# Channel means of a transformer block: two float32r passes over a split sum in place of one float32 product

## The chip, the cores and the metric

The kernel runs on one core of a Trainium2 chip. The metric is the device time of one execution in microseconds (us). The kernel before took 987.19 us, the median of three runs (986.78 to 987.68).

A core has a matrix engine (TensorE, PE in the profile; PEld is its loading of weights), a vector engine (VectorE, DVE), a scalar engine (ScalarE, ACT), a general engine (GpSimd, POOL), and queues that move data by DMA (SyncE, SP, issues most of them). Each engine takes its own instructions in one order, and waits on the others through semaphores. Matrix results land in PSUM, in banks of 128 x 512 float32.

## The reference, cut to what matters

One layer over 512 positions of 1024 channels: a normalised input is projected and goes through three mixers (a spatial gating unit, a convolution with LayerNorm, a pooling), which are merged by gates and projected; then a feed-forward part and a gated embedding follow.

```python
def rms_norm(x, g):
    y = x * lax.rsqrt(jnp.mean(x * x, axis=-1, keepdims=True) + EPS)
    return y * g
def layer_norm(x, g, b):
    mu = jnp.mean(x, axis=-1, keepdims=True)
    xc = x - mu
    var = jnp.mean(xc * xc, axis=-1, keepdims=True)
    return xc * lax.rsqrt(var + EPS) * g + b
def reference(...):
    hn = rms_norm(h, g_mix_pre)
    z_sgu, z_conv, z_pool, z_gate = jnp.split(hn @ w_in, SPLITS, axis=-1)
    br_a = spatial_gating(gelu(z_sgu), ...) @ w_sgu_out
    br_b = conformer_conv(z_conv, ...) @ w_conv_out   # GLU, conv of 31 taps, layer_norm, silu
    br_c = multiscale_pool(z_pool, ...) @ w_pool_out
    merged = gates[0] * br_a + gates[1] * br_b + gates[2] * br_c
    h = h + rms_norm(merged @ w_out, g_mix_post)
    hn = rms_norm(h, g_ffn_pre)
    f = (silu(hn @ w_gate) * (hn @ w_up)) @ w_ffn_out
    h = h + rms_norm(f, g_ffn_post)
    return h + sigmoid(h @ w_ple_gate) * (p @ w_ple)
```

## The kernel before

The activations lie transposed: channels on the 128 partitions, in eight tiles, and the 512 positions along the free dimension. A weight block of 128 outputs is loaded, split into two float32r halves (a cast on ScalarE gives the high half, a subtraction on VectorE the low half; that is `split`), and stays in TensorE while the positions stream past. Every float32 product is three float32r passes (`mm3`): high by high, high by low, low by high. Two blocks are loaded and split ahead of use; tiles `raw`, `hi`, `lo` (and `w_hi`, `w_lo` in other slots) hold them.

A norm needs a mean over the channels, and channels lie on partitions. The squares of the eight tiles are first added up (`x_sums`, `conv_sum`, `var_sum`, `o_sums`, `h_sums`, `f_sums`, each 128 partitions wide), on VectorE or POOL. Then `channel_mean` multiplies the sum by a 128 x 128 matrix of 1/1024 (`mean_mat`), which gives the mean on every partition in the one PSUM bank `ps_stat`. This is the only product in plain float32. `inv_rms` puts eight VectorE instructions behind it (`rsqrt`, tiles `x_inv`, `o_inv`, `h_inv`, `f_inv`, `conv_inv`, `rs_t`).

There are eight such means. Four have 512 positions: `x_sums` (first norm, multiplied in behind the first products `ps_first`), `conv_sum` and `var_sum` (mean and variance of the LayerNorm of the convolution, while TensorE computes the gate tiles `ps_gate`; tiles `acc` hold the convolution, `conv` its halves afterwards, which `ps_br` needs), and `h_sums` (norm ahead of the feed-forward part). Four have 256, since the norm behind the output projection (`o_sums`) and the last norm (`f_sums`) are done for each half of the positions, so that the norm and the residual of one half run beside products of the other. In the code of these two, and of the feed-forward start between them, work is written by hand in the order in which it is meant to run, inside `with order():`. Every VectorE, ScalarE and TensorE instruction written there (through `dve`, `act_e`, `pe`) is kept behind all those that were written before it. Outside, a scheduler places the instructions by a model of the time. The background taps of the convolution (`drain`) are in written order too.

In the post-norm the order is: four output tiles for all positions; the last four for the first half; the first of these for the second half; the mean of the first half; then the others, with the residual of the first half (`res.tile`) between them; a part of the feed-forward products (`ps_f`); the eight squares of h in the first half (`square_h`); the mean of the second half; its residual; and the rest of the products. In the last norm: the last tile's first half is finished, its mean taken after a few products of the second half, then the embedding products `ps_ple` with the first half's residual between them, two slices of the last product `ps_pg`, and the mean of the second half.

In the profile nearly all instructions carry line 69, the helper that records them, so tiles tell them apart; L281 is the addition of squares on POOL.

Of the kernel before, what the change touches and what calls it, by code (L numbers as in the profile page):

```python
# [8 lines left out]
F32 = mybir.dt.float32  # L9
F32R = mybir.dt.float32r  # L10
# [6 lines left out]
P = 128  # L17
T = 512
H = 256
D = 1024  # L20
# [18 lines left out]

# The first GLU pairs are multiplied before the norm of x is known.  # L40
N_RAW = 3
N_FIRST = 2 * N_RAW * P
# Matrix products on nothing that raise the tensor engine's clock while the first loads run.
N_WARM = 8
# Taps of the depthwise convolution for each tile of GLU, v, gate a, pooling, gate c; and of u.
TAPS = (4, 3, 5, 3, 5)
TAPS_U = 4
# Where a norm or a piece of a residual goes between the products, counted in k-tiles.
STAT_K, STAT_A, STAT_H, STAT_F = 4, 2, 7, 2
# [5 lines left out]
class InOrder:  # L55
    """Engines whose instructions, while `on`, are issued behind all those written before them."""

# [24 lines left out]
def hybrid_block(  # L82
# [3 lines left out]
):  # L86
    """Activations live transposed (channels on partitions, the 512 positions free), so that every
    weight is a stationary operand as it lies in memory and is loaded once. A float32 product is
    three float32r passes: each operand is split exactly into a high and a low half of 12 bits."""
    nc = tc.nc  # L90
    order = InOrder(tc)
    dve, act_e, pe = order.engine(nc.vector), order.engine(nc.scalar), order.engine(nc.tensor)

    const = ctx.enter_context(tc.tile_pool(name="const", bufs=1))
    stream = ctx.enter_context(tc.tile_pool(name="stream", bufs=3))
    wide = ctx.enter_context(tc.tile_pool(name="wide", bufs=2))
    act = ctx.enter_context(tc.tile_pool(name="act", bufs=8))
# [18 lines left out]

# [1 line left out]
    vec = const.tile([P, N_VEC + WIDTH * KT], F32, name="vec")  # L118
# [24 lines left out]

    mean_mat = const.tile([P, P], F32, name="mean_mat")
    dve.memset(mean_mat, 1.0 / D)
    warm = const.tile([P, 1], F32, name="warm")
    act_e.copy(warm, mean_mat[:, :1])
    warm_up = const.tile([P, T], BF16, name="warm_up")
# [11 lines left out]

# [1 line left out]
    def split(hi, lo, src):  # L162
# [3 lines left out]
    def split_scaled(hi, lo, src, scale):  # L166
        """The halves of src * scale, scale one number per partition."""
        act_e.activation(out=hi, in_=src, func=AF.Copy, scale=scale)
        dve.scalar_tensor_tensor(out=lo, in0=src, scalar=scale, in1=hi,
                                       op0=ALU.mult, op1=ALU.subtract)  # L170
# [34 lines left out]
    weights = Weights()  # L205
# [9 lines left out]
    def product(ps, w, acts, hs=FULL, k0=0, last=True):  # L215
        """ps[n, t] (+)= sum over the block's k of w[k, n] act[k, t]."""
        hi, lo = w
        for i, a in enumerate(acts):
            mm3(ps[:, hs], blk(hi, i), blk(lo, i), a[:, 0, hs], a[:, 1, hs],
                k0 + i == 0, last and i == len(acts) - 1)  # L220
# [7 lines left out]

# [1 line left out]
    background = []  # L230
# [6 lines left out]
    def rsqrt(y, a, t):  # L237
        """y = 1 / sqrt(a): a bit-pattern guess, a Newton step scaled by S, a third-order step."""
        dve.tensor_scalar(out=y.bitcast(I32), in0=a.bitcast(I32), scalar1=-0.5,
                          scalar2=RSQRT_SEED, op0=ALU.mult, op1=ALU.add)  # L240
        dve.tensor_tensor(out=t, in0=y, in1=y, op=ALU.mult)
        dve.scalar_tensor_tensor(out=t, in0=t, scalar=-RSQRT_C2 * RSQRT_S, in1=a,
                                 op0=ALU.mult, op1=ALU.mult)
        dve.scalar_tensor_tensor(out=y, in0=t, scalar=RSQRT_C1 * RSQRT_S, in1=y,
                                 op0=ALU.add, op1=ALU.mult)
        dve.tensor_tensor(out=t, in0=y, in1=y, op=ALU.mult)
        dve.tensor_tensor(out=t, in0=t, in1=a, op=ALU.mult)
        dve.scalar_tensor_tensor(out=t, in0=t, scalar=-10.0 / 3.0 * RSQRT_S ** 2, in1=t,
                                 op0=ALU.add, op1=ALU.mult)
        dve.scalar_tensor_tensor(out=y, in0=t, scalar=5.0 * RSQRT_S ** 4, in1=y,  # L250
                                 op0=ALU.add, op1=ALU.mult)

    def channel_mean(sums):
        """The mean over the channels of what `sums` holds by partition, on every partition."""
        ps = psum.tile([P, T], F32, tag="pst", name="ps_stat", bufs=1)
        ps = ps[:, :sums.shape[1]]
        pe.matmul(ps, lhsT=mean_mat, rhs=sums, start=True, stop=True)
        return ps

    def inv_rms(sums, y):  # L260
        """y = 1 / sqrt(mean over the channels + eps), on every partition; eps is in the sums."""
        rsqrt(y, channel_mean(sums), t2("rs_t", sums.shape[1]))
# [6 lines left out]
    def add_square(sums, src, i, engine):  # L269
        """The i-th of the squares that are summed; the second brings eps along."""  # L270
        if i == 0:
            act_e.activation(out=sums, in_=src, func=AF.Square)
        else:
            add_sq(sums, square(src), i, engine)
# [7 lines left out]

# [1 line left out]
    C_U, C_V, C_A, C_G, C_P, C_M = 0, 8, 16, 24, 32, 40  # L284
# [56 lines left out]

# [1 line left out]
    xg = [slot("br", f"xg{k}") for k in range(KT)]  # L343
    x_sums = row("x_sums")
    first = []
# [13 lines left out]

# [1 line left out]
    h_conv = [slot("cv", f"h_conv{i}", F32) for i in range(4)]  # L361
# [67 lines left out]

# [1 line left out]
    def natural(dst, evacuate, taps):  # L431
        """dst[t, block, c] from z with the positions on partitions; yields behind each block."""
        for c in range(2):
            banks = [bank("ps_nat") for _ in range(NB)]
            for kk in range(4):
                hi, lo = weights.get()
                for b in range(NB):
                    ts = slice(b * P, (b + 1) * P)
                    for j in range(2):
                        k = 2 * kk + j  # L440
                        a = hn[k]
                        ws = slice(j * T, (j + 1) * T)
                        pe.matmul(banks[b], lhsT=a[:, 0, ts], rhs=hi[:, ws],
                                         start=k == 0, stop=False)
                        pe.matmul(banks[b], lhsT=a[:, 1, ts], rhs=hi[:, ws],
                                         start=False, stop=False)
                        pe.matmul(banks[b], lhsT=a[:, 0, ts], rhs=lo[:, ws],
                                         start=False, stop=k == KT - 1)
                drain(taps)
                if kk == 3:  # L450
                    for b in range(NB):
                        evacuate(dst, b, c, banks[b])
                yield c, kk
# [73 lines left out]

# [1 line left out]
    merged = wide_tile("merged")  # L529
# [25 lines left out]

# [1 line left out]
    z_all = wide_tile("z_all")  # L557
# [44 lines left out]
    gates = []  # L602
# [12 lines left out]

# [1 line left out]
    drain(len(background))  # L617
# [31 lines left out]

    # ---- output projection, post-norm, residual; the last tiles a half of the positions at a time,  # L650
    # so that the norm of one half runs behind the product of the other ----
    o_all = wide_tile("o_all")
# [4 lines left out]
    class Residual:  # L657
        """h += o * y tile by tile, and the halves of h * scale; the low half runs a tile behind."""

# [49 lines left out]
    with order():  # L709
# [23 lines left out]

# [1 line left out]
        banks = [bank("ps_f") for _ in range(2 * N_PAIR)]  # L735
# [92 lines left out]
    with order():  # L828
# [26 lines left out]

# [1 line left out]
        w_ple_1 = weights.get(0)  # L857
# [31 lines left out]
def _blocks(w):  # L889
    """[K, N] -> [N / 128, 128, K]: one block for each 128 outputs, its k-tiles side by side."""  # L890
    k, n = w.shape
    return w.reshape(k // P, P, n // P, P).transpose(2, 1, 0, 3).reshape(n // P, P, k)


def _wide_blocks(w):
    """[1024, 1024] -> [8, 128, 1024]: for each half of the outputs, pairs of k-tiles."""
    return w.reshape(4, 2, P, 2, T).transpose(3, 0, 2, 1, 4).reshape(8, P, D)
# [54 lines left out]
```

## Time and profile before

| what | value |
|---|---|
| median of three runs | 987.19 us (986.78 to 987.68) |
| profiled execution, first to last instruction | 984.9 us |
| TensorE busy | 974.1 us (99%) |
| VectorE, ScalarE, POOL busy | 675.5, 347.1, 87.4 us |
| chain that ended last | TensorE 89%, VectorE 7% |
| granted TensorE clock | 1.000 |

The page gives busy times, the chain of waits that ended last, and the costliest groups of instructions. A row of the timeline has the start in us, the length in us, the engine, the operation, output and inputs, shapes, how many instructions were merged (x), and in brackets how long the engine had been idle before, and what ended it. A row of the chain has start, length and what was running. Products overlap in their records: how long one holds TensorE is seen from the starts that follow, or from a long stretch divided by its count. The profile has 2.3 us less than the median of the runs, since it counts from the first to the last instruction.

### The profile page before, as it was taken

Reading aid. Unit: us, or ns where it says so; the run is one execution under the profiler, and the core shown is the slowest. Engines: PE = TensorE matmul, PEld = TensorE weight load, DVE = VectorE, ACT = ScalarE, POOL = GpSimd, SP = SyncE. Lnnn points to the kernel's source line nnn. Section 1 sums busy time; section 2 is a strip of 40 time slices with the busy share of each in tenths; the row PEclk is TensorE's granted clock in tenths of the full one; section 3 lists DMA queues with packets and bytes.
Section 4 is the critical chain, followed back from the end, with each engine's and each line's share of the span. In section 5 each row is a group of like instructions: output and inputs, shape, how many; then the busy total and the mean of one; then the engine's idle time right before and its main releaser. Section 6 shows DMA issues by size and latency. Waiting matters only on the chain.

```text
span 984.9 us, 11718 instructions
## 1 busy us (share of the span) xinstructions
PE 974.1 (99%) x4682; PEld 818.4 (83%) x4682; DVE 675.5 (69%) x903; ACT 347.1 (35%) x483; POOL 87.4 (9%) x64
## 2 busy tenths in 40 slices
PE   9999999899999999999999999999999999999998
PEld 6788888688888788888888998888888888888897
DVE  7998789998988799967556687554445442223675
ACT  6422333332223332246426443332232322223442
POOL 4000004000003702160000010000000000000000
PEclk9999999999999999999999999999999999999999
DMA  6433331322222232231328102323222333334312
GB/s 226 143 107 107 109 106 65 106 69 103 86 97 86 76 128 86 102 113 65 116 99 277 65 25 74 116 86 107 88 105 87 104 84 107 93 92 141 107 43 86
DMA packets 30006, 100.53 MB, mean 102 GB/s; under 512 B 3456, under 2 KB 3968, under 8 KB 29952
## 3 DMA queue, kind: packets, MB, share of 16 engines
q1 hardware_dynamic: 29808, 99.75, 30.2%
q8 instruction: 36, 0.59, 0.2%
q14 instruction: 18, 0.15, 0.0%
q10 hardware_dynamic: 144, 0.04, 0.0%
HBM read 97.68 MB, written 2.10 MB: 101 GB/s over the span
## 4 chain that ended last, share of the span: by engine, by line
PE 89%; DVE 7%; issue 2%; DMA 1%; ACT 1%; SPq 0%; DVEq 0%; ACTq 0%
PE ps_f L69 24%; PE ps_gate L69 13%; PE ps_br L69 13%; PE ps_fo L69 12%; PE ps_ag L69 5%; PE ps_pg L69 5%; PE ps_o L69 5%; PE ps_nat L69 4%; PE ps_z L69 4%; DVE lo L69 2%; DVE acc L69 1%; PE ps_pool L69 1%; PE ps_ple L69 1%; DVE v_all L69 1%; DMA first_all<-in_w_first 1%
## 5 line engine op out<-in xcount | busy, mean ns | idle before, releaser
L69 ACT CAST hi<-raw 128x1024 fp32r<-128x1024 f32 (+3 forms) x158 | 162.5, 1030 | 455.6 <-PE ps_br L69 88.4
L69 DVE TENSOR_TENSOR lo<-raw,hi 128x1024 fp32r<-128x1024 f32 (+3 forms) x158 | 201.4, 1276 | 107.5 <-ACT hi L69 106.8
L69 DVE SCALAR_TENSOR_TENSOR acc<-h_conv,vec,acc 128x511 f32<-128x511 f32 (+14 forms) x240 | 184.2, 768 | 5.1
L69 PE MATMUL ps_f<-hg,hi 128*128 128x512 f32 (+1 forms) x624 | 184.3, 378 | 0.0
L69 PEld LDWEIGHTS ps_f<-hg,hi 128*128 128x128 f32 x624 | 115.1, 188 | 21.7
L69 PE MATMUL ps_gate<-hn,hi 128*128 128x512 f32 x384 | 119.4, 392 | 0.0
L69 PE MATMUL ps_f<-hg,lo 128*128 128x512 f32 (+1 forms) x312 | 117.8, 378 | 0.0
L69 PE MATMUL ps_fo<-f,hi 128*128 128x512 f32 (+1 forms) x396 | 110.9, 366 | 0.0
L69 PEld LDWEIGHTS ps_gate<-hn,hi 128*128 128x128 f32 x384 | 72.0, 188 | 15.9 <-issue 1.0
L69 PEld LDWEIGHTS ps_fo<-f,hi 128*128 128x128 f32 x396 | 71.7, 189 | 12.2
L69 PE MATMUL ps_nat<-hi,hn 128*128 128x512 f32 x256 | 79.0, 389 | 0.0
L69 PE MATMUL ps_gate<-hn,lo 128*128 128x512 f32 x192 | 74.8, 389 | 0.0
L69 PE MATMUL ps_fo<-f,lo 128*128 128x512 f32 (+1 forms) x198 | 72.3, 365 | 0.0
L69 PEld LDWEIGHTS ps_f<-hg,lo 128*128 128x128 f32 x312 | 58.7, 188 | 11.0
L69 PEld LDWEIGHTS ps_nat<-hi,hn 128*128 128x128 f32 x256 | 48.1, 188 | 10.0
L69 DVE TENSOR_TENSOR f<-ps_f,h_inv 128x512 f32<-128x512 f32 x22 | 15.2, 689 | 56.5 <-PE ps_f L69 56.5
L69 PE MATMUL ps_nat<-lo,hn 128*128 128x512 f32 x128 | 49.8, 389 | 0.0
L69 PE MATMUL ps_ag<-hn,hi 128*128 128x512 f32 x160 | 49.5, 390 | 0.2 <-DVE sig L69 0.2
L69 PEld LDWEIGHTS ps_gate<-hn,lo 128*128 128x128 f32 x192 | 36.1, 188 | 7.6
L69 PEld LDWEIGHTS ps_fo<-f,lo 128*128 128x128 f32 x198 | 37.3, 189 | 6.0
L69 DVE TENSOR_TENSOR silu<-ps_f,h_inv 128x512 f32<-128x512 f32 x22 | 15.2, 690 | 36.0 <-PE ps_f L69 35.9
L69 PE MATMUL ps_br<-pool,hi 128*128 128x512 f32 x128 | 39.6, 389 | 0.0
(214 smaller groups left out, 1566.1 us busy)
## 6 DMA issues: line engine op xcount, KB each, us to landing
raw<-in_w_mix SPq DMA_DIRECT2D x90, 512.0 KB, 3.2
raw<-in_w_ffn_in SPq DMA_DIRECT2D x44, 512.0 KB, 3.2
raw<-in_w_ffn_out SPq DMA_DIRECT2D x16, 448.0 KB, 3.2
raw<-in_w_ffn_out SPq DMA_DIRECT2D x8, 512.0 KB, 3.5
raw<-in_w_ple_gate SPq DMA_DIRECT2D x8, 512.0 KB, 4.1
x_all<-in_xT SPq DMA_DIRECT2D x8, 256.0 KB, 6.6
h_all<-in_xT SPq DMA_DIRECT2D x4, 512.0 KB, 5.4
out_dram<-pg SPq DMA_DIRECT2D x7, 256.0 KB, 2.0
```

The lines of the kernel that those rows point to most:

```text
L69: inst = op(*args, **kw)
```

## The change

`channel_mean` splits the sum into a high and a low float32r half by `split`, into two tiles of the six `t2` buffers, and runs two float32r passes that add up in `ps_stat`. The matrix of 1/1024 is stored as float32r; 1/1024 needs no low half. The rest of the diff takes comments and docstrings out.

```diff
-    mean_mat = const.tile([P, P], F32, name="mean_mat")
-    dve.memset(mean_mat, 1.0 / D)
+    mean_mat = const.tile([P, P], F32R, name="mean_mat")
+    dve.memset(mean_mat.bitcast(F32), 1.0 / D)
     warm = const.tile([P, 1], F32, name="warm")
-    act_e.copy(warm, mean_mat[:, :1])
+    act_e.copy(warm, mean_mat[:, :1].bitcast(F32))
...
     def channel_mean(sums):
+        n = sums.shape[1]
         ps = psum.tile([P, T], F32, tag="pst", name="ps_stat", bufs=1)
-        ps = ps[:, :sums.shape[1]]
-        pe.matmul(ps, lhsT=mean_mat, rhs=sums, start=True, stop=True)
+        ps = ps[:, :n]
+        halves = [tmp.tile([P, T], F32R, tag="t2", name="sum_half")[:, :n] for _ in range(2)]
+        split(*halves, sums)
+        for i, half in enumerate(halves):
+            pe.matmul(ps, lhsT=mean_mat, rhs=half, start=i == 0, stop=i == 1)
         return ps
```

`split`, which it now calls, is unchanged:

```python
    def split(hi, lo, src):
        act_e.copy(hi, src)
        dve.tensor_tensor(out=lo, in0=src, in1=hi, op=ALU.subtract)
```

The instructions move as follows. First ScalarE at the second half of the post-norm, before and after. `hg` are the residual's casts, `h_sums<-h_all` and `o_all<-h_all` the squares of h in the first half of the positions; the next three rows belong to the second half.

```order
L69 ACTIVATE hg_3843<-h_all,vec 128x256
L69 ACTIVATE hg_3844<-h_all,vec 128x256
L69 ACTIVATE h_sums<-h_all 128x256
L69 ACTIVATE o_all<-h_all 128x256 x7
L69 ACTIVATE hg_3837<-h_all,vec 128x256
```

```order
L69 ACTIVATE hg_3858<-h_all,vec 128x256
L69 ACTIVATE hg_3859<-h_all,vec 128x256
L69 ACTIVATE h_sums<-h_all 128x256
L69 ACTIVATE o_all<-h_all 128x256 x7
L69 CAST sum_half<-o_sums 128x256
L69 ACTIVATE hg_3852<-h_all,vec 128x256
```

The cast of the sum, which the first pass needs, comes behind all eight squares. On TensorE the two passes stand where the one product stood.

ScalarE at the second half of the last norm, after the change; `ple` are copies of the embedding products, `h_0` to `h_7` the residual's casts, first those of the first half of the positions, then those of the second:

```order
L69 ACTIVATE h_5_6113<-h_all 128x256
L69 COPY ple_6652<-ps_ple 128x512
L69 ACTIVATE h_6_6114<-h_all 128x256
L69 ACTIVATE h_7_6115<-h_all 128x256
L69 CAST sum_half<-f_sums 128x256
L69 ACTIVATE h_0_6108<-h_all 128x256
```

The cast comes behind the whole residual of the first half; nothing else moved there.

TensorE at the mean of the convolution, where the scheduler sets the order, before and after. `pool` are the tiles of the pooling branch in its last product, `hn` the tiles of the normalised input in the gate products:

```order
L69 MATMUL ps_br<-pool_2704,hi 128x512 x2
L69 MATMUL ps_br<-pool_2704,lo 128x512
L69 MATMUL ps_stat<-conv_sum,mean_mat 128x512
L69 MATMUL ps_gate<-hn_227,hi 128x512 x2
L69 MATMUL ps_gate<-hn_227,lo 128x512
```

```order
L69 MATMUL ps_gate<-hn_234,lo 128x512
L69 MATMUL ps_gate<-hn_227,hi 128x512 x2
L69 MATMUL ps_stat<-sum_half,mean_mat 128x512
L69 MATMUL ps_gate<-hn_227,lo 128x512
L69 MATMUL ps_gate<-hn_228,hi 128x512 x2
L69 MATMUL ps_gate<-hn_228,lo 128x512
L69 MATMUL ps_gate<-hn_229,hi 128x512
L69 MATMUL ps_stat<-sum_half,mean_mat 128x512
```

The passes moved from the place directly behind the pooling branch to the second gate tile, behind 26 gate products, with five products between them. The passes for the variance moved likewise, to 85 products behind these; at the start, the first pass for `x_sums` stands eight products later than the old one, and the conv products of the first three `ps_br` tiles are interleaved.

## The prediction

> **What bounds the kernel now.** I read the page first (busy shares, chain by engine), then the chain in order of time, then each of the eight places where a channel mean is taken, engine by engine in the timeline.
>
> ```profile
> span 984.9 us, 11718 instructions
> PE 974.1 (99%) x4682; PEld 818.4 (83%) x4682; DVE 675.5 (69%) x903; ACT 347.1 (35%) x483; POOL 87.4 (9%) x64
> PE 89%; DVE 7%; issue 2%; DMA 1%; ACT 1%; SPq 0%; DVEq 0%; ACTq 0%
> ```
>
> TensorE is the bound: 89% of the chain. A product that TensorE no longer runs is worth its own time; a wait that TensorE did not have before costs its own time. The next four rows, from the chain in order of time (start, length, what), give the prices on TensorE.
>
> ```profile
> 426.41 0.86 PE ps_stat L69 x2
> 471.70 43.52 PE ps_br L69 x192
> 551.37 0.43 PE ps_stat L69 x2
> 551.80 8.63 PE ps_o L69 x72
> ```
>
> A float32 mean holds TensorE for 0.86 us at 512 positions and 0.43 us at 256 (two records each). A float32r pass takes 43.52/192 = 0.227 us at 512 and 8.63/72 = 0.120 us at 256. Two passes are 0.45 and 0.24, so each mean saves 0.41 or 0.19 us. There are four of each: 2.4 us at most, 0.24% of the span. That is all that the change can win.
>
> **What it adds.** Each mean now needs a cast on ScalarE and, behind it, a subtraction on VectorE before TensorE can run the second pass. TensorE, ScalarE and VectorE each take their work in the order written in the post-norm, feed-forward and last part, so what counts is what stands ahead of the cast. I take the eight means one by one; times are those of the profiled execution.
>
> *First half of the post-norm* (timeline of the three engines, start and length; the last row is a cast of the same size elsewhere):
>
> ```profile
> 549.31 0.43 DVE L69 TENSOR_TENSOR o_sums<-o_sums,o_sq 128x256 f32<-128x256 f32 x1 [2.45 <-ACT o_sq L69]
> 551.21 0.59 PE L69 MATMUL ps_stat<-o_sums,mean_mat 128*128 128x256 f32 x2
> 551.78 0.38 ACT L69 ACTIVATE o_sq<-ps_o 128x256 f32<-128x256 f32 x1
> 927.75 0.42 ACT L69 ACTIVATE h<-h_all 128x256 fp32r<-128x256 f32 x1
> ```
>
> The sum is ready at 549.74, so the old mean starts at once. The new cast stands behind the copy and the square of the tile that TensorE has just finished: the square ends at 552.16, the cast (0.42) at about 552.5, the subtraction (0.42, by the 0.43 of the first row) at 552.95. With a hop of 0.06 and the second pass of 0.12, the next product starts at 553.13 instead of 551.21 + 0.42 = 551.63: **+1.5 us**. The residual that hangs on it moves along with TensorE.
>
> *Second half of the post-norm:*
>
> ```profile
> 561.25 0.43 DVE L69 TENSOR_TENSOR o_sums<-o_sums,o_sq 128x256 f32<-128x256 f32 x1 [0.26 <-ACT o_sq L69]
> 564.59 0.59 PE L69 MATMUL ps_stat<-o_sums,mean_mat 128*128 128x256 f32 x2
> 567.69 2.24 ACT L69 ACTIVATE o_all<-h_all 128x256 f32<-128x256 f32 x7
> 568.72 5.21 POOL L281 TENSOR_TENSOR h_sums<-h_sums,o_all 128x256 f32<-128x256 f32 x6 [124.54 <-ACT o_all L69]
> 568.92 0.82 DVE L69 TENSOR_TENSOR rs_t<-o_inv 128x256 f32<-128x256 f32 x1
> 569.77 0.42 DVE L69 SCALAR_TENSOR_TENSOR rs_t<-rs_t,ps_stat 128x256 f32<-128x256 f32 x1
> ```
>
> Here the sum is ready at 561.68, three microseconds early, but on ScalarE the cast is written behind the residual and the eight squares of h, whose last seven end at 569.93. The cast then ends at 570.3, the subtraction at 570.75, and TensorE goes on at about 570.9 instead of 564.59 + 0.42 = 565.01: **+5.9 us**. This is the largest term. None of that chain waits for TensorE, so a TensorE delay elsewhere does not shorten it. The POOL row runs beside the subtraction, and beside it a VectorE multiplication took 0.82 where the row below it took 0.42; so the term may be 6.3. Nothing follows from it on VectorE: its second reciprocal starts 2.6 us later, while the products that need its result come 5.9 us later.
>
> *The two halves of the last norm:*
>
> ```profile
> 919.35 0.42 DVE L69 TENSOR_TENSOR f_sums<-f_sums,sq 128x256 f32<-128x256 f32 x1 [1.31 <-ACT sq L69]
> 919.83 0.70 PE L69 MATMUL ps_stat<-f_sums,mean_mat 128*128 128x256 f32 x2 [0.22 <-DVE f_sums L69]
> 920.61 0.28 PE L69 MATMUL ps_fo<-f,lo 128*128 128x256 f32 x1
> 925.30 0.42 DVE L69 TENSOR_TENSOR f_sums<-f_sums,sq 128x256 f32<-128x256 f32 x1 [1.09 <-ACT sq L69]
> 938.10 0.59 PE L69 MATMUL ps_stat<-f_sums,mean_mat 128*128 128x256 f32 x2
> 940.24 0.42 ACT L69 ACTIVATE h<-h_all 128x256 fp32r<-128x256 f32 x1 [0.83 <-DVE h_all L69]
> ```
>
> First half: TensorE already waits here. Cast and subtraction add about 0.9 us behind 919.77; second pass and hop end at 920.83. Before, the first product behind the mean started two passes ahead of the row at 920.61, at 920.37: **+0.5**. Second half: the sum is ready at 925.72, but the cast stands behind the casts of the residual, the last of which ends at 940.66. Cast to 941.0, subtraction to 941.45, next product at 941.63 instead of 938.52: **+3.1**.
>
> *Feed-forward norm and first norm:*
>
> ```profile
> 594.14 0.69 DVE L69 TENSOR_SCALAR h_inv<-ps_stat 128x512 int32<-128x512 int32 x1 [5.18 <-PE ps_stat L69]
> 24.67 1.02 PE L69 MATMUL ps_stat<-x_sums,mean_mat 128*128 128x512 f32 x2
> 26.32 1.05 ACT L69 CAST hi<-raw 128x1024 fp32r<-128x1024 f32 x1 [5.71 <-DMA raw<-in_w_mix]
> 27.41 1.23 DVE L69 TENSOR_TENSOR lo<-raw,hi 128x1024 fp32r<-128x1024 f32 x1 [1.40 <-ACT hi L69]
> 44.02 0.62 ACT L69 CAST hn<-nrm 128x512 fp32r<-128x512 f32 x1 [3.05 <-DVE nrm L69]
> 43.90 0.68 DVE L69 TENSOR_TENSOR hn<-nrm,hn 128x512 fp32r<-128x512 f32 x1
> 45.91 0.30 PEld L69 LDWEIGHTS ps_ag<-hn,hi 128*128 128x128 f32 x2 [0.67 <-DVE sig L69]
> ```
>
> h: VectorE had waited 5.18 us for this mean, and the split needs 0.62 + 0.68, so it hides: **-0.4** (the 5.9 us of TensorE above only widen the cover; without cover it would cost 1.3 more). x: the first pass now stands eight products later, at 26.5, but its cast is queued behind the cast of a weight that lands at 26.32, and ends at 27.37 + 0.5 = 27.9. TensorE stands 1.4 us, saves 0.4, and is 1.0 late until it meets the wait at 45.9 that it has anyway, some 0.5 us: **+0.55** (0.1 to 1.1). VectorE fits the 0.68 into a gap of 0.53 between two weight splits, and its own chain stays within 0.2 us.
>
> *The two means of the convolution's LayerNorm:*
>
> ```profile
> 427.48 4.86 DVE L69 TENSOR_TENSOR acc<-acc,ps_stat 128x512 f32<-128x512 f32 x8
> 432.58 1.05 ACT L69 CAST hi<-raw 128x1024 fp32r<-128x1024 f32 x1
> 434.22 9.96 POOL L281 TENSOR_TENSOR var_sum<-var_sum,sq 128x512 f32<-128x512 f32 x6 [5.29 <-ACT gate_b L69]
> 454.87 4.91 DVE L69 TENSOR_TENSOR acc<-acc,conv_inv 128x512 f32<-128x512 f32 x8
> 469.28 2.50 DVE L69 TENSOR_TENSOR conv<-acc,conv 128x512 fp32r<-128x512 f32 x4 [1.19 <-ACT conv L69]
> ```
>
> Here the order is the scheduler's, and it puts the passes behind 26 gate products: the second ends at 426.25 + 32 x 0.227 = 433.7 (26 products, two passes, five between). Centring starts at 434.0 instead of 427.48. Its 4.9 us, one addition (0.7) and POOL's 9.96 bring the variance to 449.4, the split to 450.8, and the passes, placed 85 products further, end at 454.1 without a wait. Reciprocal and two weight splits that now fall inside it put the scaling at 462.7 instead of 454.87, and the last halves near 480 instead of 471.8. TensorE wants the first of them at 470.7. The new order interleaves the first three tiles: 3 tiles x 5 slices x 3 passes = 45 products, 10.2 us, need none of the last three halves, which covers the gap of 9.3 us but not each arrival on the way. I estimate 1.5 us of waiting (0 if all fits, 9.3 if nothing covers), near the low end because of the interleaving: 1.5 - 0.8 = **+0.7**.
>
> **Sum.** 1.5 + 5.9 + 0.5 + 3.1 - 0.4 + 0.55 + 0.7 = +11.8 us. On the profiled span this is 984.9 + 11.8 = 996.7. The runs shown have a median of 987.2, 2.3 us more than that span, and nothing in the change touches those 2.3; so **999.0 us**.
>
> **Rivals.** *The clock falls in the long gap* (30%). TensorE would stand from 564.59 to 570.3. The start shows what a rested array does (matmuls grouped in the windows 8 to 9 us and 10 to 12 us), and the last row the longest wait in the middle of the program:
>
> ```profile
> L69 PE MATMUL ps_first<-xg,first 128*128 128x512 f32 x4 | 1.9, 626 | 0.0
> L69 PE MATMUL ps_first<-xg,first 128*128 128x512 f32 x11 | 2.7, 389 | 0.0
> PE ps_tr L69 <- DVE gated L69: 3.2, 2, 1.6
> ```
>
> A pass of 626 ns instead of 389 until about 9 us, though products began at 1.3: up to 7.8 us at half pace, 3.9 lost. Gaps of 1.6 us bring no such thing back; whether 5.7 us do, no row shows. With the middle of 0 and 3.9 the time is 1001.0, at most 1002.9. [...]
>
> *The LayerNorm chain is not covered* (13%): if TensorE meets each half of the conv tiles late, half of the 9.3 us shows, 3 more than I took: 1002. For it speaks that the old chain ended at 471.8 with no slack against 471.70; against it the interleaving.
>
> *The waits do not form, and only the shorter passes count* (5%): if ScalarE had the casts done when TensorE arrives, that is if the new waits together stay below 2.4 us, the time falls to 984.8. For it: both long waits are for sums that are ready 3 and 12 us early. Against it: the rows of the order place the cast behind the squares and behind the residual, and neither engine passes an instruction by. That would also be the case in which the change does not do what the order says; a few of the waits forming would end near no change.
>
> **How the numbers follow.** The forecast as summed has 52%, with +-2 us for the LayerNorm and the first norm (997 to 1001). The clock and the LayerNorm rival lie above, to 1004; the low end of 995 allows for half of the smaller waits hiding. A difference of 0.2% (2 us) is what a measurement of this kernel tells from none. Faster by that 3%, within it 3%, slower 94%.
>
> **What would show it.** Right: in the new profile TensorE idles before the mean of the second post-norm half by 5 to 6.5 us with ScalarE's seven squares directly ahead of the cast, before that of the last norm's second half by about 3, before the first post-norm half by 1.3; DVE's wait for the h mean stays; TensorE's busy time falls by some 2 us. Wrong: those casts start before the squares, or matmuls behind the gap at 565 take over 500 ns (the clock rival), or a wait of over 4 us at the first conv products.

## Result and profile after

| kernel | median us | range | executions |
|---|---|---|---|
| before | 986.99 | 986.58 to 987.68 | 4 |
| changed | 1003.36 | 1003.16 to 1003.52 | 4 |

The changed kernel takes 1.0164 times as long (95% interval 1.0151 to 1.0176): 16.4 us more. The forecast was 999.0 (995 to 1004), slower with a chance of 0.94.

The page of the changed kernel:

```profile
span 1001.7 us, 11727 instructions
PE 977.1 (98%) x4682; PEld 820.7 (82%) x4682; DVE 679.7 (68%) x911; ACT 353.0 (35%) x493; POOL 87.8 (9%) x64
PE 86%; DVE 7%; ACT 4%; issue 2%; DMA 1%; SPq 0%; DVEq 0%; ACTq 0%
```

TensorE is still the bound, but its share of the chain fell from 89% to 86%, ScalarE's rose from 1% to 4%, and TensorE's busy time rose by 3.0 us. The waits of TensorE (total, times, longest) name the reason for the first:

```profile
PE ps_stat L69 <- ACT sum_half L69: 13.3, 5, 5.5
```

TensorE waits 13.3 us for casts of sums, where in the kernel before it waited 0.2 us for a sum in all. Where the span grew is read from the chain in order of time: the same stretch of products starts in both kernels, and the difference of the starts is how far the changed one has fallen behind. Before:

```profile
404.64 21.77 PE ps_br L69 x96
...
515.22 36.15 PE ps_o L69 x216
...
565.18 28.07 PE ps_f L69 x234
...
594.11 208.90 PE ps_f L69 x930
...
920.53 3.95 PE ps_fo L69 x33
...
938.69 42.26 PE ps_pg L69 x288
```

After:

```profile
407.16 21.76 PE ps_br L69 x96
...
518.64 36.16 PE ps_o L69 x216
...
556.77 8.65 PE ps_o L69 x72
...
576.28 30.42 PE ps_f L69 x234
...
607.16 208.90 PE ps_f L69 x930
...
934.18 3.95 PE ps_fo L69 x33
...
955.53 42.27 PE ps_pg L69 x288
```

| place | behind at its end | added here | forecast |
|---|---|---|---|
| first norm (to the pooling branch's last tiles) | 2.52 | +2.5 | +0.55 |
| LayerNorm | 3.42 | +0.9 | +0.7 |
| post-norm, first half | 4.97 | +1.55 | +1.5 |
| post-norm, second half | 11.10 | +6.1 | +5.9 |
| 234 feed-forward products behind it, and the mean of h | 13.05 | +2.35 and -0.4 | 0 and -0.4 |
| last norm, first half | 13.65 | +0.6 | +0.5 |
| last norm, second half | 16.84 | +3.2 | +3.1 |

The row of before for the first half of the post-norm, 551.80, stands in the prediction. Five of the seven rows came within 0.25 us. Two did not: the start, and the feed-forward products, which took 30.42 us for the 234 that had taken 28.07. The timeline of the second half of the post-norm, TensorE, ScalarE, VectorE:

```profile
575.24 1.04 PE L69 MATMUL ps_stat<-sum_half,mean_mat 128*128 128x256 f32 x2 [5.52 <-ACT sum_half L69]
...
572.66 2.23 ACT L69 ACTIVATE o_all<-h_all 128x256 f32<-128x256 f32 x7
574.80 0.39 ACT L69 CAST sum_half<-o_sums 128x256 fp32r<-128x256 f32 x1
...
575.22 0.43 DVE L69 TENSOR_TENSOR sum_half<-o_sums,sum_half 128x256 fp32r<-128x256 f32 x1 [1.71 <-ACT sum_half L69]
```

The seven squares run into the cast, the cast into the first pass: the wait of 5.52 us is made by what stands ahead of the cast on ScalarE. The squares are 2.5 us of that; ahead of them stand the last casts of the residual, for each of which ScalarE itself waits 0.89 us for VectorE. The subtraction took 0.43 us, so POOL's additions did not double it. The same picture stands at the second half of the last norm, where the cast starts right behind the last cast of the residual, with a wait of 2.74 us:

```profile
954.64 0.89 PE L69 MATMUL ps_stat<-sum_half,mean_mat 128*128 128x256 f32 x2 [2.74 <-ACT sum_half L69]
...
954.20 0.39 ACT L69 CAST sum_half<-f_sums 128x256 fp32r<-128x256 f32 x1
```

The short waits, at the first halves of the two norms and at the first convolution tile (there the products between 477.1 and 482.3 us start late by some 1.6 us in all, counted from their starts; the row shows the longest piece):

```profile
555.92 0.85 PE L69 MATMUL ps_stat<-sum_half,mean_mat 128*128 128x256 f32 x2 [1.13 <-ACT sum_half L69]
...
933.33 0.84 PE L69 MATMUL ps_stat<-sum_half,mean_mat 128*128 128x256 f32 x2 [0.66 <-ACT sum_half L69]
...
478.19 0.50 PE L69 MATMUL ps_br<-conv,hi 128*128 128x512 f32 x1 [0.68 <-ACT conv L69]
```

At the start TensorE waits 3.22 us, and then the five products between the two passes start 0.43 us apart instead of 0.227:

```profile
28.27 0.54 PE L69 MATMUL ps_stat<-sum_half,mean_mat 128*128 128x512 f32 x1 [3.22 <-ACT sum_half L69]
28.61 2.33 PE L69 MATMUL ps_first<-xg,first 128*128 128x512 f32 x5
...
26.65 1.04 ACT L69 CAST hi<-raw 128x1024 fp32r<-128x1024 f32 x1 [5.43 <-DMA raw<-in_w_mix]
27.60 0.61 ACT L69 CAST sum_half<-x_sums 128x512 fp32r<-128x512 f32 x1
```

So behind the two longest waits TensorE is slow. The table of windows (stretch, its length, TensorE busy and matmuls, granted clock, then DMA) says what it is; the stretches lie as a finer table shows the clock to change. First the start, then the post-norm:

```profile
25.16:28.58 3.42, 0.31 (x1) 1.00 0.85 302
28.58:31.99 3.41, 3.41 (x9) 0.50 0.80 253
31.99:35.40 3.41, 3.41 (x16) 1.00 0.85 238
```

```profile
567.88:571.29 3.41, 1.84 (x16) 1.00 0.00 0
571.29:574.71 3.42, 0.00 (x0) 1.00 0.00 0
574.71:578.12 3.41, 2.88 (x12) 0.50 0.00 0
578.12:581.53 3.41, 3.41 (x18) 0.50 0.00 0
```

The granted clock is one half for one stretch of 3.41 us at the start, and for two behind the long wait; from 581.53 on the products take 0.12 us each again. This is the rival "the clock falls in the long gap", at the place that it named and at one that it did not. It also explains most of the longer busy time: passes were saved, but a product at half pace counts as busy for longer, 2.35 us in the 234 products alone.

The profiled execution was granted 0.995 of the clock over its span, the other three 0.993. By an estimate (3.41 us at half clock are 0.0017 of this span) that is one more such stretch in each; no trace shows where.

### The profile page after: what moved, and what is told of

Its sections match the earlier page's. It is cut to its first block, busy times and chain, and to the rows that moved or that the text cites. A ratio compares the mean times of both kernels' runs of the same rounds, so it can differ in the third digit from the quotient of the medians.

```text
span 1001.7 us, 11727 instructions
## 1 busy us (share of the span) xinstructions
PE 977.1 (98%) x4682; PEld 820.7 (82%) x4682; DVE 679.7 (68%) x911; ACT 353.0 (35%) x493; POOL 87.8 (9%) x64
## 4 chain that ended last, share of the span: by engine, by line
PE 86%; DVE 7%; ACT 4%; issue 2%; DMA 1%; SPq 0%; DVEq 0%; ACTq 0%
PE ps_f L69 24%; PE ps_br L69 12%; PE ps_gate L69 12%; PE ps_fo L69 12%; PE ps_ag L69 5%; PE ps_o L69 4%; PE ps_nat L69 4%; PE ps_pg L69 4%; PE ps_z L69 4%; DVE lo L69 2%; DVE acc L69 2%; PE ps_first L69 2%; PE ps_pool L69 1%; DVE v_all L69 1%; DMA x_all<-in_xT 1%
## 5 line engine op out<-in xcount | busy, mean ns | idle before, releaser
L69 PE MATMUL ps_br<-conv,hi 128*128 128x512 f32 x128 | 39.7, 392 | 0.8 <-ACT conv L69 0.7
L69 PE MATMUL ps_f<-hg,w_hi 128*128 128x256 f32 (+1 forms) x176 | 40.2, 322 | 0.0
```

What stands on the lines that cost most here:

```text
L69: inst = op(*args, **kw)
```

## Experiments

The theory: each wait is made by what stands ahead of the cast on ScalarE, not by the split or the passes; and long waits bring the clock down, which is paid behind them. The rivals: the split and two passes cost the time wherever they stand; and the slow products come from something else than TensorE's idleness. All kernels compute the whole reference. In the diffs, `split_sum` makes the two halves, and `channel_mean` takes halves that exist already.

**One split early.**

```diff
                     add_mixed(*sqs.pop(0), hi_half)
+                    if i == N_HALF - 1 and not sqs:
+                        o_hi = split_sum(o_sums[:, hi_half])
...
-        inv_rms(o_sums[:, hi_half], y)
+        inv_rms(o_sums[:, hi_half], y, halves=o_hi)
```

> Only the place of one split changes: the cast and the subtraction for the second half of the post-norm are written directly behind the last addition of that sum, between two tiles of the first half's residual, and the two passes stay where they were. Theory (the wait is made by what stands ahead of the cast on ScalarE, and the long gap brings the clock down): TensorE no longer waits at this mean, so the +6.1 us there become -0.2, and the half-pace stretch behind it (+2.35 us) goes too: 1003.4 - 6.3 - 2.35 = 994.7 us. If the clock falls for another reason than the gap, the 2.35 us stay: 997. Rival (the split and the two passes cost the time wherever they stand, or the later residual of the first half now holds the products back): 1001 to 1003.

Measured: 995.03 us (994.02 to 997.08), 1.0083 of before (1.0066 to 1.0100). ScalarE's cast and TensorE's passes in this kernel:

```profile
565.64 0.41 ACT L69 CAST sum_half<-o_sums 128x256 fp32r<-128x256 f32 x1
...
568.52 0.40 PE L69 MATMUL ps_stat<-sum_half,mean_mat 128*128 128x256 f32 x2
```

The cast is three microseconds ahead of the pass, no wait is left at this mean, and the 234 products behind it run 28.07 us as before the change. Moving one cast and one subtraction, 0.4 us each, took back 8.3 us in the median. The same split and the same passes are still there, so the rival that they cost the time falls for this place. Two surprises stand in the same trace: the start had a wait of only 2.33 us, yet the clock fell, and it now fell also behind the last norm's wait of 2.74 us, where it had not in the changed kernel:

```profile
25.05:28.46 3.41, 1.28 (x6) 1.00 0.86 247
28.46:31.87 3.41, 3.41 (x10) 0.50 0.84 244
...
943.23:946.65 3.42, 1.61 (x11) 1.00 0.00 0
946.65:950.06 3.41, 3.41 (x18) 0.50 0.00 0
```

**Work on nothing in the gap.** Extra bf16 products that nothing uses stand ahead of the two passes; the cast stays late.

```diff
+        for _ in range(fill):      # 20, and 8 in the second kernel
+            pe.matmul(ps, lhsT=warm_up[:, :P], rhs=warm_up, start=True, stop=True)
```

> In the gap of 5.5 us ahead of the mean of the second post-norm half TensorE gets 20 extra bf16 products of 512 positions that nothing uses, in the bank of the mean (about 4.5 us at 0.227 each); the cast stays where it was, so the mean comes at the same time. Theory (idleness of TensorE lowers its clock): idle of about 1 us is left, the feed-forward products behind it run at full pace, and 2.35 us are saved: 1001.0 us. Rival (the slow stretch comes from something else that runs there, such as POOL's additions or the reciprocal beside the products): the products still take 0.21 instead of 0.12 us each until 581, and the time stays 1003.4.

Measured: 1000.65 us (1000.06 to 1001.23), 1.0137 (1.0122 to 1.0152). The wait shrank to 1.19 us, and the 234 products behind took 28.07 us:

```profile
568.81 4.26 PE L69 MATMUL ps_stat<-warm_up 128*128 128x512 bf16 x19
574.27 0.84 PE L69 MATMUL ps_stat<-sum_half,mean_mat 128*128 128x256 f32 x2 [1.19 <-ACT sum_half L69]
```

The row has 19 of the 20 extra products. The mean comes at the same place in the stream (0.97 us earlier, as the whole stream of this profile does from the start on) and 2.7 us are gone in the median, of which the trace puts 2.35 into these products. With 1.19 us of idleness in place of 5.5 the clock did not fall here, though POOL, the reciprocal and the place are all unchanged: at this mean it went with the idleness and not with them.

> The same with 8 extra products, which leave 3.7 us of idleness directly ahead of the mean. If any gap above about 3 us lowers the clock (the 3.2 us at the first norm did, the 2.7 us at the last norm did not), the half-pace stretch is still there and the time is 1003.0 to 1003.4 us. If the loss grows with the length of the gap, a part of the 2.35 us goes: about 1002.3. If a gap must be near 5 us in this place, all of it goes: 1001.0.

Measured: 1002.49 us (1001.99 to 1003.54), 1.0157 (1.0142 to 1.0172). The wait was 3.78 us, the clock fell behind it for 6.8 us, and the 234 products took 30.20 us, 0.2 less than in the changed kernel. So here a wait of 3.8 us cost nearly as much clock as one of 5.5. The rest of the 0.9 us came from the start, where this profile shows a wait of 2.13 us and no fall. The median alone would have fitted the second case of the expectation, a loss that grows with the gap; the trace shows that it was not so.

**The first norm back to float32.**

```diff
-            inv_rms(x_sums, x_inv)
+            inv_rms(x_sums, x_inv, plain=True)
```

> The mean of the first norm goes back to one float32 product, the other seven stay as changed. Theory (the wait for the cast and the lower clock behind it cost 2.5 us at the start, and this runs through to the end): TensorE has no wait of 3.2 us at 25 us, no half-pace stretch behind it, and the time is 1003.4 - 2.5 = 100​0.9 us. Rival (the start is bound elsewhere, by VectorE's halves for the first products, and what is lost is given back at the wait that stood at 45.9 us before): 1002.8 to 1003.4.

Measured: 1002.43 us (1001.58 to 1002.87), 1.0154 (1.0139 to 1.0169). Only 0.9 us came back in the median where the theory had 2.5, so its size was wrong. The trace has no wait and no fall at 25 us, but its stream still stood 0.91 us behind the first profile of before at the pooling branch. And the clock elsewhere behaved differently: behind the wait of 5.52 us it was low for one stretch, not two,

```profile
566.58:569.99 3.41, 1.53 (x13) 1.00 0.00 0
569.99:573.40 3.41, 0.00 (x0) 1.00 0.00 0
573.40:576.81 3.41, 3.17 (x13) 0.50 0.00 0
```

and it fell behind the last norm's 2.74 us. These two cancel to 0.1 us. That left a question on the start, for which the kernel before was profiled again.

> The kernel before, unchanged, for a second profile. If the start differs between executions by the moment at which the first projection weight lands (26.3 us in the first profile, 25.6 to 27.3 in the four runs with other means), the lag that its TensorE stream has behind the first profile at the end of the pooling branch equals the difference of that moment within 0.3 us. If the moment does not matter, the two profiles agree there within 0.3 us whatever it is.

Measured: 987.12 us, one execution. The first projection weight is cast at 26.74 instead of 26.32 us, and the stream is 0.48 us later than in the first profile:

```profile
26.74 1.05 ACT L69 CAST hi<-raw 128x1024 fp32r<-128x1024 f32 x1 [6.29 <-DMA raw<-in_w_mix]
...
405.12 21.77 PE ps_br L69 x96
```

In these two profiles the start follows the moment at which this weight lands (0.42 us later, the stream 0.48), and that differs between executions of one kernel. Taking it away gives the cost of the split at the start without that luck (each row from the same two rows of its own profile):

| profile | weight cast at | ps_br at | difference | clock fell at the start |
|---|---|---|---|---|
| before, twice | 26.32, 26.74 | 404.64, 405.12 | 378.32, 378.38 | no |
| x mean in float32 | 27.12 | 405.55 | 378.43 | no |
| two passes: 8 extra products | 27.34 | 406.25 | 378.91 | no |
| two passes: LayerNorm in float32 (below) | 27.53 | 406.48 | 378.95 | no |
| two passes: changed kernel | 26.65 | 407.16 | 380.51 | yes |
| two passes: one split early | 25.56 | 406.12 | 380.56 | yes |
| two passes: 20 extra products | 25.60 | 406.19 | 380.59 | yes |

The split and its wait cost 0.55 us, the fall of the clock 1.6 us more, and 0.3 of the changed kernel's 2.5 were the weight.

The rows with a fall have something else in common: there the first products reach full pace earlier. In the first profile of before their starts are 0.43 us apart until 9.2 us, in the one with 8 extra products until 10.0 us, and in the one with the LayerNorm in float32, by an estimate from the 0.33 us by which it came later to the mean, for some half a microsecond more; in the three with a fall they run at full pace, 0.227 us apart, from 5.5 to 5.7 us on. So TensorE reached the mean at 24.8 to 25.05 us instead of 26.8 and 27.2, and waited 2.33 to 3.22 us instead of 2.13 and 1.99. The early pace alone does not move the difference: two kernels below, which by an estimate from where they reached this mean also have it (23.48 us, and 26.97 behind 18 products more, against 24.67 in before), but have no wait there (the version that beats both, and all splits early), have 378.39 and 378.40. What it went with is a longer wait at the start, 2.33 to 3.22 us.

**The LayerNorm back to float32.**

```diff
-    ps_mu = channel_mean(conv_sum)
+    ps_mu = channel_mean(conv_sum, plain=True)
...
-    inv_rms(var_sum, conv_inv)
+    inv_rms(var_sum, conv_inv, plain=True)
```

> The two means of the LayerNorm go back to one float32 product each, the other six stay as changed. Theory (the scheduler's later passes delay the halves of the convolution, and TensorE waits 0.7 us more and saves 0.8 at the passes): from the end of the pooling branch to the first output product the time is again that of the kernel before, 0.9 us shorter than in the changed kernel, and the time is 1002.4 us. Rival (these two means cost nothing): 1003.4.

Measured: 1001.49 us (1001.25 to 1002.17), 1.0148 (1.0134 to 1.0162). From the pooling branch's last tiles to the first output product the trace has 110.58 us, as in before (515.22 - 404.64), against 111.48 after: the 0.9 us are there. The rest of the difference to the changed kernel lies where executions differ: in this profile the clock did not fall at the start, was low for less of the work behind the wait of 5.52 us (29.17 us for the 234 products), and fell behind the last norm.

**All splits early.** All eight means stay two passes. Early are the four splits that made TensorE wait by more than 1 us; those of the LayerNorm, of h and of the last norm's first half stay where they were. Beside the split moved above, `split_sum` is called behind the last addition to the first half of `o_sums`, behind the last addition to `f_sums`, and behind that to `x_sums`; there the casts of the next weights are kept behind it, and the passes of the first norm stand at the fifth k-tile instead of the fourth:

```diff
+    x_halves = split_sum(x_sums)
+    with order():
+        weights.ahead(2)
...
-STAT_K, STAT_A, STAT_H, STAT_F = 4, 2, 7, 2
+STAT_K, STAT_A, STAT_H, STAT_F = 5, 2, 7, 2
```

> All eight means stay two float32r passes, but the splits are written as soon as their sum is ready: both halves of the post-norm, the second half of the last norm, and the first norm, where the split stands ahead of the casts of the next weights and its passes come one k-tile (18 products) later. Theory (the whole loss is waits for casts that stand behind other work, and the lower clock that such waits bring): no wait of TensorE at a mean above 0.7 us, granted clock 0.999 to 1.000, and against the kernel before: post-norm -0.2 and -0.2, h -0.4, last norm +0.6 and -0.2, LayerNorm +0.9, first norm about 0, so 987.0 + 0.5 = 987.5 us (986.5 to 989, since the first weight lands at a moment that differs by 1 us between executions). Rival (the casts, subtractions and passes themselves cost several us whatever their place): 990 or more.

Measured: 987.37 us (986.74 to 988.75, 11 executions), before beside it 987.01: 1.0003 (0.9994 to 1.0012). The granted clock is 0.999 to 1.000, and one wait for the cast of a sum is left, in the first half of the last norm:

```profile
PE ps_stat L69 <- ACT sum_half L69: 0.7, 1, 0.7
```

The chain of this kernel around the post-norm, to be set against the rows of before:

```profile
516.02 36.15 PE ps_o L69 x216
...
552.40 8.63 PE ps_o L69 x72
...
565.59 28.07 PE ps_f L69 x234
...
594.12 208.90 PE ps_f L69 x930
```

From `ps_o` to the next `ps_o` 36.38 us where before had 36.58, then 13.19 to `ps_f` where before had 13.38, then 28.53 where before had 28.93: -0.20, -0.19 and -0.40, the savings of the shorter passes, now visible. The 16.0 us that came back were in the order of the casts and in the clock; the LayerNorm's 0.9 us and the last norm's 0.6 are still there, and the shorter passes pay for them.

**One late cast alone.** The kernel with all splits early, with one of them put back to its late place: that of the post-norm's second half, then that of the last norm's second half.

> The kernel with all splits early, but the split for the second half of the post-norm stands behind the eight squares again, as in the changed kernel: this one late cast alone. Theory (the clock is judged in fixed windows of about 3.41 us, and falls to half for the next window when TensorE was busy in less than some 40% of one): the wait is 5.5 us, it always contains enough of one window, so the clock falls; the half-pace stretch is 3.4 or 6.8 us long as the window edges lie, and costs 1.0 to 2.4 us. Time 987.4 + 6.3 + 1.0 to 2.4 = 994.7 to 996.1 us. Rival (the loss depends on the length of the gap alone): always 2.35, 996.1. If the waits don't add up one by one, below 994 or above 997.

Measured: 995.84 us (995.51 to 997.75), 1.0086 (1.0071 to 1.0101): 8.5 us above 987.37 for one cast in the wrong place, or 8.0 when each kernel is set against the executions of before beside it (987.49 and 987.01). In the profile 6.3 are the wait and 1.6 the clock, which was low for two stretches, from 569.13 to 575.97 us, but TensorE waited until 571.36. The time alone (the rival had 996.1) would not separate the two; the traces do. In the four profiles that have this same wait of 5.52 us the 234 products behind it took 0.97 (x mean in float32), 1.10 (LayerNorm in float32), 1.62 (here) and 2.35 us (changed kernel) more than 28.07.

> The kernel with all splits early, but the split for the second half of the last norm stands behind the residual of the first half again: this one late cast alone. Theory: the wait is 2.7 us and costs 3.4 us against the early split. Whether the clock falls depends on how the wait lies in the windows: cut in two with TensorE busy in more than 48% of each, nothing; mostly in one window, so that TensorE is busy in less than 38% of it, half pace for 3.4 us behind the wait, 1.4 us more. Time 990.8 or 992.2 us, and executions may differ in it. Rival (a fixed threshold in the length of the gap, above 2.7 us): always 990.8.

Measured: 992.58 us (990.10 to 993.29), 1.0042 (1.0029 to 1.0054). The six executions fall in two groups by the clock that each was granted: 990.10 and 991.03 us at 1.000, and 992.25, 992.91, 993.14 and 993.29 us at 0.997 to 0.998. That fits a program in which the same wait has the fall in some executions and not in others, but it is not shown: only the one of 993.29 us was traced, and the kernel before, which has no such wait, also has executions at 0.997 and 0.998. A fixed threshold in the length of the wait is excluded by the traces themselves: this wait of 2.74 us is followed by a fall in four profiles (one split early, x mean in float32, LayerNorm in float32, this one) and by none in three (changed kernel, 20 and 8 extra products). The profiled execution of this kernel:

```profile
941.39:944.80 3.41, 1.75 (x12) 1.00 0.00 0
944.80:948.22 3.42, 3.42 (x18) 0.50 0.00 0
```

and here are the two stretches that share the same wait in the changed kernel, where it did not:

```profile
950.17:953.59 3.42, 1.73 (x15) 1.00 0.27 109
953.59:957.00 3.41, 2.24 (x16) 1.00 0.00 0
```

The first of these two rows shows TensorE busy 1.73 us without a fall behind it, the first row of the other kernel 1.75 us with one: read from this column, the expectation's bounds of 38% and 48% busy do not hold (1.75 and 1.73 are both 51%, and the 1.53 of the kernel with the x mean in float32, 45%, had no fall either). The last section has a count that comes closer.

**A version that beats both.** Two passes where the split is covered (both halves of the post-norm, the feed-forward norm, both halves of the last norm), the first norm and the LayerNorm in float32, and six instead of three k-tiles ahead of the first mean of the last norm:

```diff
-        product(halves[1], (hi, lo), f_T[c0:c0 + 3], hi_half, c0, False)
+        product(halves[1], (hi, lo), f_T[c0:c0 + 6], hi_half, c0, False)
```

> float32r passes with early splits only where a split is covered: both halves of the post-norm, the feed-forward norm, and both halves of the last norm, the first of them with three more k-tiles ahead of the mean, so that TensorE does not wait for it; the first norm and the LayerNorm go back to one float32 product, in the order of the kernel before. Theory: post-norm -0.2 and -0.2, h -0.4, last norm -0.4 and -0.2, sum -1.4: 985.6 us, at the edge of what can be measured. Rival (the later residuals of the first halves, behind the splits on VectorE, make TensorE wait): 988 or more, with a new wait for the halves of h in one of the two places.

Measured: 985.49 us (985.25 to 986.84, 11 executions), 0.9986 of before (0.9978 to 0.9995). The interval lies below 1, so the gain is measured, but it is 0.14% and smaller than the 2.3 us by which executions of the kernel before differ among themselves; the theory had 1.4 us for these five places. No wait for the halves of h appeared in the two places that the rival named.

## Why the prediction was right, and where it was not

- *The time*: the forecast as summed, 997 to 1001 with 52%, was missed. 1003.36 lies in the stated range of 995 to 1004 only because of the clock rival, and above that rival's own upper price of 1002.9. On the profiled spans the miss is 5.0 us (1001.7 against 996.7): 2.35 and 1.6 are two falls of the clock, 0.3 a weight that landed later, and 0.7 the small misses of the other terms. The medians show only 4.4 because the sum added 2.3 us between span and median. Each execution on record with its span is about 1.8 us longer than its own span; the other 0.5 was that the profiled execution was a short one, so the reason given there for the 2.3 is only in part right, and 0.5 us of the miss was hidden by luck.
- *The sign and the mechanism* were right: 2.4 us at most to win, and casts that stand behind other work on ScalarE. Putting the casts where their sums are ready took the whole loss back (987.37), and one late cast alone cost 8.5 us.
- *Second half of the post-norm, +5.9*: +6.1, seven squares directly ahead of the cast. *First half, +1.5*: +1.55. *Last norm, +0.5 and +3.1*: +0.6 and +3.2. *h, -0.4*: -0.4, with VectorE waiting 10.9 us for this mean. *LayerNorm, +0.7*: +0.9, confirmed by taking it back; the 1.5 us of waiting are 1.6 to 1.7 in the trace, but they had been picked from a span of 0 to 9.3 by the interleaving alone, so that the size is partly luck (its 32 products are 33; the 433.7 is right). The doubt that POOL would double the subtraction was empty: 0.43 us, with POOL's additions running beside it.
- *First norm, +0.55*: measured +2.5. The step that failed is "TensorE stands 1.4 us". It reached the mean at 25.05 and not at 26.5, and stood 3.22 us, because in this execution the first products ran at full pace from 5.5 us on and not from 9.2 as in the profile that the step was worked out from. In the two profiles of two passes in which full pace came later, with 8 extra products at 10.0 us, it reached the mean at 26.8 and 27.2, near the 26.5 of the step, and there the cost is 0.55 us by the table of the start, as the sum said. What the step did not ask about is the clock behind the wait: +1.6, and 0.3 from a weight that landed later.
- *The clock rival*, 30%: it happened. Its price of 0 to 3.9 us with the middle at 1.95 compares with 2.35 us in the products behind the gap; that the middle came so near is in part luck, since it stands between no fall and the 7.8 us of half pace at the start, while the falls behind waits lasted 3.41 us or twice that. The mis-sized part is the number of places: the working priced one gap, and there were three long ones, 3.22, 5.52 and 2.74 us, with a fall behind the first two in the profiled execution. The sign set for this rival, matmuls of over 500 ns behind the gap, would have missed it: at 256 positions the products at half pace are recorded with 410 ns against 283 at full. The prediction asked how long the gap is; a gap of 2.33 us was followed by a fall (one split early) and one of 2.74 us was not (the changed kernel). One stretch of half clock at the start cost 1.6 us, two behind the long wait 2.35.
- *TensorE's busy time falls by 2 us*: it rose by 3.0, mostly since products at half pace count as busy.
- *Not covered LayerNorm* and *waits do not form* did not happen.

## What to carry to other kernels

When an operation is cut into parts for several engines, ask for each part what is written ahead of it on its engine, and issue it when its input is ready, not where its result is used: here that was worth 16 us against 2.4 us of shorter products. A long wait of the matrix engine was paid twice here, once as the wait and once as half pace behind it (6.3 and 1.6 us for one late cast). Before comparing two kernels by single profiles, take out what differs between executions anyway, here the landing of a first weight and the fall of the clock.

## What the runs showed of the hardware that was not expected

**Half clock came in stretches of one length.** Apart from the first microseconds, where products start 0.43 us apart while the granted clock reads 1.00 (before, until 9.2 us), and the tail of the program, every stretch of half clock in these profiles lasted 3.41 us or twice that. Within an execution the edges lie on one grid: in the kernel with one split early the clock fell at 28.46 and at 946.65 us, 918.19 us apart, 269 stretches of 3.413; in the changed kernel at 28.58 and 574.71, 546.13 us apart, 160 of 3.413; with the x mean in float32 at 573.40 and 952.28, 378.88 us apart, 111 of 3.413. In these traces the falls went with how little TensorE worked in the stretch of 3.41 us on that grid just ahead. The clock fell behind stretches with 0.00, 0.31, 1.28, 1.61 and 1.75 us of recorded work, and stayed behind stretches with 1.53 (x mean in float32, 566.58 us), 1.64 (8 extra products, at the start), 1.73 and 1.84; between 1.5 and 1.8 us both happen. The recorded time counts the tail of the last product of a stretch, though. An estimate from the starts gives a clearer line: each product counts for its pace (0.120 us at 256 positions, 0.227 at 512, 0.11 for the short products of `ps_tr`, from 0.44 us for four in the chain), and for its part where it lies across an edge. Counted so, in all twelve profiles and apart from the first microseconds and the tail, no stretch at full clock with more than 1.39 us is followed by half clock, and none with less than 1.38 by full clock: the 1.75 us become 1.39, the 1.61 become 1.24, and the 1.53, 1.64 and 1.73 that kept the clock become 1.38, 1.50 and 1.56. So by this estimate the line between the two lies near 1.4 us of 3.41 in these profiles; no run was made to test it. From half, the clock came back behind a stretch with 3.17 us of work (the x mean in float32), and did not behind one with 2.88 (the changed kernel). The length of a wait alone does not tell: 2.33 us (one split early) had a fall behind it, and 2.74 us (the changed kernel) had none.

**The first weight lands at different moments.** Its cast starts at 25.56 to 27.53 us over the profiles of this case, and in those without a fall at the start `ps_br` stands 378.32 to 378.95 us behind that cast.
